# A decoder trunk on one core: the Strassen chunks of the down projections are loaded once, split and summed in one place

## The chip, the cores and the metric

The kernel runs on one core of a Trainium2 chip, which has eight. The metric is the device time of one execution in microseconds. The engines that matter are PE (matrix products), DVE (elementwise arithmetic), ACT (copies and activations) and SP, which only issues transfers from memory. Each engine runs its own list of instructions in the order in which the program emitted them.

## The reference

Two layers over 256 tokens of width 1024, in float32. Each layer has a token mixer (a chunked gMLP in the first, block attention in the second), a normalization, a gated feed-forward with a causal convolution, and a second normalization. The change lies in the feed-forward's last product, the down projection:

```python
def conv_ffn(x, w_up, conv_w, conv_b, w_down):
    S = x.shape[1]
    h = x @ w_up                       # 256 x 1024 times 1024 x 5632
    hp = jnp.pad(h, ((0, 0), (CONV_WIDTH - 1, 0), (0, 0)))
    hc = conv_b
    for j in range(CONV_WIDTH):
        hc = hc + conv_w[j] * hp[:, j:j + S]
    g, val = jnp.split(hc, 2, axis=-1)
    return (jax.nn.gelu(g) * val) @ w_down     # 256 x 2816 times 2816 x 1024
```

## The kernel before

**Products.** Every float32 operand is split into two parts, a high part `hi` in the matmul's own format (a copy by ACT) and a low part `lo`, the rest (a subtraction by DVE); `split` (L339) records the two. A product is the sum of three matmuls: hi times hi, hi times lo, lo times hi. All weights come from memory, are split on arrival and used once. So each chunk of weights costs a transfer, ACT copies and DVE subtractions, then PE time.

**Chunks.** `stream` (L349) lists all weight chunks in the order of use: `f_up0` (22 chunks), `f_dn0` (11), the attention's, `f_up1` (22), `f_dn1` (11). A chunk is 128 partitions x 2048 columns (1 MB); a chunk of a down projection holds two slices k = 2c and 2c + 1 of the contraction, 1024 output columns each. `prep(i)` (L470) records a chunk's load into one of two `raws` tiles and its splits into `whi` and `wlo`, rings that hold five chunks. `spent(name, c)` (L500) is called when chunk c has been used and calls `prep` for the chunk five further on.

**The Strassen chunks.** In each down projection four chunks, 3, 5, 6 and 7 (`FAST`, L54), are multiplied by `unit` (L706) in Strassen's way. The chunk is a 2 x 2 matrix of blocks (B11, B12 are the halves of slice 2c, B21, B22 of slice 2c + 1), the tokens are two halves, and seven block products (21 matmuls of 512 columns) stand for eight (24). They need
- the plain blocks B11 and B2 (B21 and B22 together), split into `whi`, `wlo`: for these `prep` loads 512 and 1024 columns of the chunk into a `raws` tile;
- four sums of blocks, the weight forms: `load_sums` (L431) loads the whole chunk a second time, into two places of the scratch tile `ff` (0 to 1023 and 2560 to 3583 for the first and third of the four, 1024 to 2047 and 3584 to 4607 for the second and fourth), and `weight_forms` (L438) adds blocks there in place (one DVE instruction of 1024 elements, two of 512) and splits the four sums into the `xt` tiles (first and third) or into used-up columns of `rr` (second and fourth). When it is done it records the load of the chunk two further on, into the same place;
- sums of token blocks, `token_forms` (L459), in `small`.

The scratch tile `ff` also serves `conv_up` (L891), the up projection with its gate: `joined` (2560 and 3584, 1024 columns each, in turn) and `grings` (0 to 2047) hold a pass's values, two chunks in a pass, until its result is split into `rr`.

**Order.** `project_out` (L683) goes through chunks 0 to 7 in order, both token tiles in each, and through the last three chunks (`TAIL`) one output piece after another: 18 matmuls, six slices, for each of the four pieces. The forms of chunk 3 are recorded at its start, those of chunks 5 and 6 after chunk 3, those of 7 after chunk 5 (`more`, L764). `combine` (L741) adds the products that belong to the units once chunk 7 is done. `ln_rows` (L541) loads the scale and shift rows of the next normalization into the one tile `lnrow`, at the start of the projection; the tile also holds the attention's values later.

**The planner.** Nothing is issued while this is recorded. `Plan` (L84) collects operations with estimated costs, the buffers that they read and write, and a due time worked back from PE's order; `emit` (L129) runs a list schedule with those costs (a load lands 1100 ns plus its bytes at 415 GB/s after its issue) and then emits every engine's instructions in the order of start times. So the costs and due times fix the order of DVE, ACT and SP beforehand, while the real waits are those of semaphores. PE's main products keep the order in which they were recorded.

Of the kernel before, what the change touches and what calls it, by code (L numbers as in the profile page):

```python
# [18 lines left out]
P = 128  # L19
# [32 lines left out]
REST = 25000  # L52
AHEAD = 12000
FAST = {"f_dn0": (3, 5, 6, 7), "f_dn1": (3, 5, 6, 7)}  # L54

# [173 lines left out]
def trunk_kernel(ctx: ExitStack, tc: tile.TileContext, a: dict, out: bass.AP):  # L231
# [25 lines left out]
    def place(which, at, cols):  # L257

        t = rr if which == "rr" else ff
        prev = [b for s, e, b in owners[which] if s < at + cols and at < e]  # L260
        b = Buf(t[:, at:at + cols], prev)
        owners[which] = [x for x in owners[which] if not (at <= x[0] and x[1] <= at + cols)] + [(at, at + cols, b)]
        return b
# [61 lines left out]
    def tt(o, x, y, op, r, w):  # L325
        dve(70 + 1.04 * flat(x), lambda: nc.vector.tensor_tensor(o, x, y, op=op), r, w)  # L326
# [8 lines left out]
    def load(o, src, w, r=(), nbytes=None, rank=None):  # L335
        nbytes = nbytes or flat(o) * P * 4
        plan.op("sp", nbytes / 415.0, lambda: nc.sync.dma_start(o, src), r, w, nbytes=nbytes, rank=rank)
# [38 lines left out]

    xrows = [Buf(t) for t in xs_]

    def raw_of(i):
        if i == 2:  # L380
            early = place("ff", 2560, CH)
        elif i == 3:
            return [(b, b.ap, 0) for b in xrows]
        else:
            early = raws.new()
        return [(early, early.ap[:, s * SUB:(s + 1) * SUB], s * 4) for s in range(2)]
# [4 lines left out]
    def used_up(k0, k1):  # L391

        if "spare" in inner:
            inner["spare"] = [Buf(b.ap, [b]) for b in inner["spare"]]
            return inner["spare"]
        bufs = []
        for b in inner["rr"]:
            n = Buf(b.ap[:, k0 * S:k1 * S], [Buf(None)])
            n.prev[0].ops = [o for k in range(k0, k1) for o in [b.wr[k], *b.rd.get(k, ())]]
            bufs.append(n)  # L400
        inner["spare"] = bufs
        return bufs
# [22 lines left out]
    def is_fast(i):  # L425
        name, c = stream[i]
        return c in FAST.get(name, ())

    raw_sums = {}

    def load_sums(name, j):  # L431

        key = name, FAST[name][j]
        raw_sums[key] = [place("ff", o + SUB * (j % 2), SUB) for o in (0, 5 * HALF)]
        for n, b in enumerate(raw_sums[key]):
            load(b.ap, a[name][key[1]][:, n * SUB:(n + 1) * SUB], [(b, range(2))])

    def weight_forms(name, j):  # L438

        key = name, FAST[name][j]  # L440
        r0, r1 = raw_sums[key]
        f = ff.rearrange("p (a n) -> p a n", n=HALF)
        b11 = 2 * (j % 2)
        b12, b21, b22 = b11 + 1, b11 + 5, b11 + 6
        h, l = xt_new() if j % 2 == 0 else used_up(0, KT)
        tt(f[:, b22:b12 - 1:-5, :], f[:, b12:b12 + 1, :].to_broadcast([P, 2, HALF]),
           f[:, b22:b11 - 1 if b11 else None:-6, :], ALU.add, [(r0, [0, 1]), (r1, [1])], [(r0, [1]), (r1, [1])])
        tt(f[:, b11, :], f[:, b22, :], f[:, b11, :], ALU.add, [(r0, [0]), (r1, [1])], [(r0, [0])])
        tt(f[:, b21, :], f[:, b11, :], f[:, b21, :], ALU.add, [(r0, [0]), (r1, [0])], [(r1, [0])])
        for n, raw in ((1, r1), (0, r0)):  # L450
            parts, sl = [2 * n, 2 * n + 1], slice(n * SUB, (n + 1) * SUB)
            split((h, parts, h.ap[:, sl]), (l, parts, l.ap[:, sl]), (raw, [0, 1], raw.ap))
        forms[key] = h, l
        if j + 2 < len(FAST[name]):
            load_sums(name, j + 2)

    tokens = {}

# [11 lines left out]
    def prep(i):  # L470
        name, c = stream[i]
        raw = raw_of(i)
        if is_fast(i):
            for o, n in ((0, HALF), (SUB, SUB)):
                load(raw[0][0].ap[:, o:o + n], a[name][c][:, o:o + n], [(raw[0][0], range(o // 256, (o + n) // 256))])
        elif name != "a_v":
            load(raw[0][0].ap, a[name][c], [(raw[0][0], range(8))])
        for _, _, s, e in [h for h in HEAD if h[:2] == (name, c)]:
            b, v, p0 = raw[s // SUB]
            o = s % SUB  # L480
            load_head(v[:, o:o + e - s], [(b, range(p0 + o // 256, p0 + (o + e - s) // 256))], name, c, s)
        subs = []
        for s in range(2):
            hi, lo = whi.new(), wlo.new()
            rb, rv, p0 = raw[s]
            pieces = [(0, HALF)] if is_fast(i) and not s else [(0, 256), (256, 512), (512, 1024)] if not i + s else [(0, 512), (512, 1024)] if name == "a_v" or i in FINE else [(0, SUB)]
            for b, e in pieces:
                split((hi, range(b // 256, e // 256), hi.ap[:, b:e]), (lo, range(b // 256, e // 256), lo.ap[:, b:e]),
                      (rb, range(p0 + b // 256, p0 + e // 256), rv[:, b:e]))
            subs.append((hi, lo))  # L490
        chunks[i] = subs
# [8 lines left out]
    def spent(name, c):  # L500
        i = where[name, c] + CHUNKS
        if i < len(stream):
            prep(i)
# [10 lines left out]
    def xt_new():  # L514
        return xth.new(), xtl.new()
# [166 lines left out]

    def project_out(name, nk, at, xold, li, rows_i, wait=REST, first=None):  # L683

        rows = None if name == "b_o" else ln_rows(rows_i)
        last, fine = li is None, name not in ("a_out", "f_dn0", "b_o")


# [68 lines left out]
                done_with(b, 0)  # L757

        if units:
            load_sums(name, 0)  # L760
            if len(units) > 1:
                load_sums(name, 1)
            weight_forms(name, 0)
        def more(c):  # L764

            for j, after in enumerate([None, KT // 2 - 1, *units[:2]]):
                if c == after and j < len(units):
                    weight_forms(name, j)

        for k, t in order:  # L770
            if k // 2 in units:
                if k % 2 == t == 0:
                    unit(k // 2)
                elif k % 2 and t:
                    spent(name, k // 2)
                    more(k // 2)
                    if k // 2 == units[-1]:
                        combine()
                continue
            step(t, k, pieces[t][:1])  # L780
            step(t, k, pieces[t][1:], last=nk - 1 if t == 0 or not fine else nk - NARROW - 1)
            if t and k % 2:
                spent(name, k // 2)
                if units:
                    more(k // 2)
# [106 lines left out]
    def conv_up(layer, h, l):  # L892
# [50 lines left out]
        for i in range(2, FT, 2):  # L943
            whole, four = four_banks()
            cols_times([(b, *sub(name, i + j // 2, j % 2)) for j, b in enumerate(four)], h, l)
            for n in range(2):
                spent(name, i + n)
            c = joined.new()
            c3, b3 = (x.rearrange("p (a n) -> p a n", a=4) for x in (c.ap, whole))
            act(c3, b3[:, :, S:], AF.Copy, four, [c], psum=True)  # L950
            tt(c3, b3[:, :, :S], c3, ALU.add, [*four, c], [c])
            gv = [r.new() for r in grings]
            for n in range(2):
                for j in range(2):
                    o, d = c3[:, 2 * n + j, :], gv[j].ap[:, n * S:(n + 1) * S]
                    cw, dp = cc[:, layer, j * FT + i + n, :], (gv[j], [n])
                    act(d, o, AF.Identity, [c, convc], [dp], bias=cw[:, 3:4], scale=cw[:, 2:3])
                    for e in (1, 2):
                        stt(d[:, e:], o[:, :S - e], cw[:, 2 - e:3 - e], d[:, e:], ALU.mult, ALU.add, [c, dp, convc], [dp])
            key, both = (f"f_dn{layer}", i // 2), [0, 1]  # L960
            g = gv[0]
            if key[1] in FAST.get(key[0], ()):
                g = kept[key] = place("ff", 4608 + HALF * (FAST[key[0]].index(key[1]) % 3), HALF)
            act(g.ap, gv[0].ap, AF.Gelu_apprx_tanh, [(gv[0], both)], [(g, both)], table="gelu")
            tt(g.ap, g.ap, gv[1].ap, ALU.mult, [(g, both), (gv[1], both)], [(g, both)])
            at = slice(i * S, (i + 2) * S)
            split((ah, [i, i + 1], ah.ap[:, at]), (al, [i, i + 1], al.ap[:, at]), (g, both, g.ap))
            if key in kept and key[1] in FAST[key[0]][:2]:
                token_forms(key)
        return lambda k, t: (av[:, k, t * P:(t + 1) * P], lv[:, k, t * P:(t + 1) * P], [(ah, [k]), (al, [k])])  # L970


# [221 lines left out]
```

## Time and profile before

| what | value |
|---|---|
| median of three runs | 563.64 us (563.34 to 566.98) |
| the profiled execution's own time | 569.39 us |
| its span | 567.7 us |
| busy PE, DVE, ACT | 553.3, 509.2, 374.8 us |
| moved by DMA | 117.40 MB |
| f_up0's last matmuls end, f_dn0 begins | 202.4 us |
| f_up1's last matmuls end, f_dn1 begins | 496.8 us |

How to read it: times are microseconds from the start of the span. A row of the timeline or of the chain gives start, length, engine, line of the kernel, operation, destination, source and the number of instructions; in brackets stands how long the engine had been idle before it and what released it. A row of a window gives, for each engine, busy time and in brackets the number of instructions that touch the window, then the clock that PE was granted (1.00 is full), the share of the DMA engines' time, and GB/s. A row of a wait gives total, number and longest. In the rows of groups the mean length of one instruction, in ns, stands behind the busy total. Most operations are recorded by helpers: L308 is every product, L320 ACT's copies and activations, L326 DVE's additions and subtractions, L330 its fused operations, L337 a load on the SP queue, L314 a transposition.

### The profile page before, as it was taken

The numbers are of one execution on the slowest core, as the hardware profiler recorded it, in microseconds if no ns is written. First come the engines' busy times: TensorE is split into PE (matmuls) and PEld (weight loads), VectorE is DVE, ScalarE is ACT, GpSimd is POOL, SyncE is SP. The second block draws the span as 40 slices with busy tenths as digits, with TensorE's granted clock in tenths as the row PEclk, the third lists the DMA queues.
The fourth block names the chain that finished last, engine by engine and source line by source line (L and its number), as shares of the span: only waits on it lengthen the run. The fifth ranks groups of instructions, "written<-read, shape, count | busy, mean of one in ns | idle before, by whom it ended". The sixth has DMA issues, their size and how long they took to land.

```text
span 567.7 us, 8102 instructions
## 1 busy us (share of the span) xinstructions
PE 553.3 (97%) x2959; PEld 470.8 (83%) x2959; DVE 509.2 (90%) x891; ACT 374.8 (66%) x627; POOL 11.8 (2%) x17
## 2 busy tenths in 40 slices
PE   8999999999999999999999999999999999999794
PEld 6888888998988988778888887788898898988684
DVE  5898899999999998998958888889999999997987
ACT  6746678688787772555667877487787778673510
POOL 0110010000000000001000000000000000000001
PEclk9999999999999999989999999999999999999888
DMA  8986545775545557574475544426766455566602
GB/s 319 405 297 252 177 145 218 276 291 199 199 152 219 204 190 268 173 260 148 162 282 186 186 169 149 185 82 234 285 253 222 180 218 196 169 214 214 207 13 74
DMA packets 23559, 117.40 MB, mean 207 GB/s; under 512 B 2640, under 2 KB 5984, under 8 KB 12384
## 3 DMA queue, kind: packets, MB, share of 16 engines
q1 hardware_dynamic: 22944, 116.24, 56.6%
q10 hardware_dynamic: 576, 0.66, 0.3%
q8 instruction: 23, 0.38, 0.2%
q14 instruction: 16, 0.13, 0.1%
HBM read 115.81 MB, written 1.07 MB: 206 GB/s over the span
## 4 chain that ended last, share of the span: by engine, by line
PE 78%; DVE 9%; DMA 8%; issue 3%; ACT 2%; SPq 0%; DVEq 0%; ACTq 0%
PE bank L308 75%; DMA ff<-in_f_dn 5%; DVE ff L326 4%; PE bank L314 2%; DMA raw<-in_f_dn 2%; DVE wlo L326 2%; DVE ff L330 1%; DVE rr L326 1%; ACT whi L320 1%; DMA raw<-in_head 1%; ACT xt L320 0%; DVE x L330 0%; DVE xt L326 0%; ACT rr L320 0%; DVE small L326 0%
## 5 line engine op out<-in xcount | busy, mean ns | idle before, releaser
L320 ACT ACTIVATE whi<-raw 128x1024 fp32r<-128x1024 f32 (+2 forms) x209 | 188.0, 935 | 87.0 <-DMA raw<-in_f_dn 28.6
L326 DVE TENSOR_TENSOR wlo<-raw,whi 128x1024 fp32r<-128x1024 f32 (+2 forms) x209 | 217.5, 1069 | 17.4 <-ACT whi L320 16.4
L308 PE MATMUL bank<-xt,whi 128*128 128x512 f32 x832 | 195.8, 391 | 0.0
L308 PEld LDWEIGHTS bank<-xt,whi 128*128 128x128 f32 x832 | 154.2, 188 | 30.7
L308 PE MATMUL bank<-whi,rr 128*128 128x512 f32 (+1 forms) x392 | 125.5, 391 | 3.3 <-DVE rr L326 3.3
L308 PE MATMUL bank<-xt,wlo 128*128 128x256 f32 x832 | 104.7, 283 | 0.0
L308 PEld LDWEIGHTS bank<-xt,wlo 128*128 128x128 f32 x832 | 103.0, 192 | 2.1
L308 PEld LDWEIGHTS bank<-whi,rr 128*128 128x128 f32 x392 | 73.6, 189 | 18.9 <-DVE rr L326 4.0
L308 PE MATMUL bank<-wlo,rr 128*128 128x512 f32 (+1 forms) x196 | 76.0, 388 | 0.0
L330 DVE SCALAR_TENSOR_TENSOR ff<-ff,convc 128x255 f32<-128x255 f32 (+1 forms) x160 | 67.1, 478 | 0.1
L308 PE MATMUL bank<-whi,xt 128*128 128x512 f32 (+1 forms) x196 | 62.4, 400 | 1.1 <-ACT whi L320 1.1
L326 DVE TENSOR_TENSOR ff<-ff 128x512 f32<-128x512 f32 (+3 forms) x76 | 45.0, 615 | 8.4 <-DMA ff<-in_f_dn 8.4
L320 ACT ACTIVATE ff<-bank 128x256 f32<-128x256 f32 (+3 forms) x66 | 39.6, 617 | 19.3 <-PE bank L308 19.0
L320 ACT ACTIVATE ff<-ff,convc 128x256 f32<-128x256 f32 x80 | 42.3, 591 | 13.8 <-DVE ff L326 13.1
L308 PEld LDWEIGHTS bank<-whi,xt 128*128 128x128 f32 x196 | 37.6, 196 | 9.6 <-ACT whi L320 2.1
L308 PEld LDWEIGHTS bank<-wlo,rr 128*128 128x128 f32 x196 | 37.1, 189 | 7.3
L326 DVE TENSOR_TENSOR ff<-bank,ff 128x256 f32<-128x256 f32 (+2 forms) x50 | 37.5, 769 | 1.8 <-ACT ff L320 1.8
L308 PE MATMUL bank<-wlo,xt 128*128 128x512 f32 (+1 forms) x98 | 36.9, 392 | 0.0
L320 ACT ACTIVATE rr<-ff 128x512 fp32r<-128x512 f32 (+2 forms) x36 | 24.5, 692 | 15.7 <-DVE ff L326 15.7
L320 ACT ACTIVATE ff<-bank,lncol 128x128 f32<-128x128 f32 x48 | 18.8, 459 | 17.5 <-PE bank L314 17.4
L326 DVE TENSOR_TENSOR rr<-ff,rr 128x512 fp32r<-128x512 f32 (+2 forms) x36 | 27.4, 773 | 1.4 <-ACT rr L320 1.4
L326 DVE TENSOR_TENSOR xt<-ff,xt 128x256 fp32r<-128x256 f32 (+2 forms) x31 | 21.6, 702 | 2.3 <-ACT xt L320 2.0
(70 smaller groups left out, 373.8 us busy)
## 6 DMA issues: line engine op xcount, KB each, us to landing
raw<-in_f_up SPq DMA_DIRECT2D x44, 1024.0 KB, 4.8
raw<-in_f_dn SPq DMA_DIRECT2D x14, 1024.0 KB, 4.9
ff<-in_f_dn SPq DMA_DIRECT2D x16, 512.0 KB, 4.7
raw<-in_b_qk SPq DMA_DIRECT2D x8, 1024.0 KB, 4.8
lnrow<-in_lnrow SPq DMA_DIRECT2D x5, 1024.0 KB, 6.6
raw<-in_a_u SPq DMA_DIRECT2D x4, 1024.0 KB, 8.5
raw<-in_a_out SPq DMA_DIRECT2D x4, 1024.0 KB, 5.1
raw<-in_f_dn SPq DMA_DIRECT2D x8, 512.0 KB, 4.7
```

Of the source, the lines that this page charges most:

```text
L308: nc.tensor.matmul(o, l, x, start=start, stop=stop, skip_group_check=mixed)
L314: nc.tensor.transpose(o, x, ident.ap)
L320: plan.op("act", ns, lambda: nc.scalar.activation(o, x, func, **kw), r, w, table=table)
L326: dve(70 + 1.04 * flat(x), lambda: nc.vector.tensor_tensor(o, x, y, op=op), r, w)
L330: lambda: nc.vector.scalar_tensor_tensor(o, x, s, y, op0=op0, op1=op1), r, w)
```

## The change

Each of the eight Strassen chunks is loaded once, in two halves of 512 KB, into a home of its own; the plain blocks are split from there, and the sums are then formed in place there. `HOMES` names the home of each of the four: the place of ff that held the first and third chunk's copy, the one of the second and fourth, the tile `lnrow`, and the first one again. So chunk 3 lies in home 0, chunk 5 in home 1, chunk 6 in `lnrow`, chunk 7 in home 0 once chunk 3's forms are split. `prep` records these loads; `load_sums` is gone. `FORMS` says for each of the four which tiles take its forms and after which chunk they are recorded; both are as before. The first sum, which overwrites B12 and B22, waits until B22's plain split has read; the sum over B11 waits for B11's. The rows of the second normalization are loaded after `combine` is recorded instead of at the projection's start. In `conv_up` the two calls of `spent` stand at the end of a pass instead of after its products.

```diff
+HOMES = (0, 1, 2, 0, 1)
+FORMS = ((0, None), (1, 3), (0, 3), (1, 5))
...
+    def home(i):
+        name, c = stream[i]
+        j = HOMES[FAST[name].index(c)]
+        if j < 2:
+            pair, t, at = [place("ff", o + SUB * j, SUB) for o in (0, 5 * HALF)], ff, (0, 1, 5, 6)
+            at = [x + 2 * j for x in at]
+        else:
+            old, t, at = rowring.held[0], rowring.tiles[0], (0, 1, 2, 3)
+            group = rowring.held[0] = Buf(old.ap, [old])
+            pair = [Buf(old.ap[:, n * SUB:(n + 1) * SUB], [old]) for n in range(2)]
+            for b in pair:
+                b.ops = group.ops
+        raw_sums[name, c] = pair, t.rearrange("p (a n) -> p a n", n=HALF), at
+        return [(b, b.ap, 0) for b in pair]
+
     def raw_of(i):
+        if is_fast(i):
+            return home(i)
...
-    def load_sums(name, j):
-        key = name, FAST[name][j]
-        raw_sums[key] = [place("ff", o + SUB * (j % 2), SUB) for o in (0, 5 * HALF)]
-        for n, b in enumerate(raw_sums[key]):
-            load(b.ap, a[name][key[1]][:, n * SUB:(n + 1) * SUB], [(b, range(2))])
...
     def weight_forms(name, j):
         key = name, FAST[name][j]
...
-        h, l = xt_new() if j % 2 == 0 else used_up(0, KT)
+        (r0, r1), f, (b11, b12, b21, b22) = raw_sums[key]
+        left, right, both = (range(2), range(2, 4), range(4))
+        h, l = used_up(0, KT) if FORMS[j][0] else xt_new()
...
         forms[key] = h, l
-        if j + 2 < len(FAST[name]):
-            load_sums(name, j + 2)
...
         if is_fast(i):
-            for o, n in ((0, HALF), (SUB, SUB)):
-                load(raw[0][0].ap[:, o:o + n], a[name][c][:, o:o + n], [(raw[0][0], range(o // 256, (o + n) // 256))])
+            for n, (b, _, _) in enumerate(raw):
+                load(b.ap, a[name][c][:, n * SUB:(n + 1) * SUB], [(b, range(4))])
...
-        rows = None if name == "b_o" else ln_rows(rows_i)
+        rows = None if name == "b_o" or name in FAST else ln_rows(rows_i)
...
         if units:
-            load_sums(name, 0)
-            if len(units) > 1:
-                load_sums(name, 1)
             weight_forms(name, 0)
...
                     if k // 2 == units[-1]:
                         combine()
+                        rows = ln_rows(rows_i)
...
             cols_times([(b, *sub(name, i + j // 2, j % 2)) for j, b in enumerate(four)], h, l)
-            for n in range(2):
-                spent(name, i + n)
             c = joined.new()
...
                 token_forms(key)
+            for n in range(2):
+                spent(name, i + n)
```

More of the change, by code (lines that the diff above doesn't have):

```diff
@@ L377, in trunk_kernel @@
     xrows = [Buf(t) for t in xs_]
+    raw_sums = {}
+    def home(i):
[12 more added lines that the diff above has]
+        return [(b, b.ap, 0) for b in pair]
     def raw_of(i):
+        if is_fast(i):
+            return home(i)
         if i == 2:
@@ L427, in is_fast @@
         return c in FAST.get(name, ())
-    raw_sums = {}
-    def load_sums(name, j):
-        key = name, FAST[name][j]
-        raw_sums[key] = [place("ff", o + SUB * (j % 2), SUB) for o in (0, 5 * HALF)]
-        for n, b in enumerate(raw_sums[key]):
-            load(b.ap, a[name][key[1]][:, n * SUB:(n + 1) * SUB], [(b, range(2))])
     def weight_forms(name, j):
         key = name, FAST[name][j]
[L441 to L444, printed above, removed]
-        h, l = xt_new() if j % 2 == 0 else used_up(0, KT)
[L446 to L449, printed above, removed]
+        (r0, r1), f, (b11, b12, b21, b22) = raw_sums[key]
+        left, right, both = (range(2), range(2, 4), range(4))
+        h, l = used_up(0, KT) if FORMS[j][0] else xt_new()
+        tt(f[:, b22:b12 - 1:b12 - b22, :], f[:, b12:b12 + 1, :].to_broadcast([P, 2, HALF]),
+           f[:, b22:b11 - 1 if b11 else None:b11 - b22, :], ALU.add, [(r0, both), (r1, right)], [(r0, right), (r1, right)])
+        tt(f[:, b11, :], f[:, b22, :], f[:, b11, :], ALU.add, [(r0, left), (r1, right)], [(r0, left)])
+        tt(f[:, b21, :], f[:, b11, :], f[:, b21, :], ALU.add, [(r0, left), (r1, left)], [(r1, left)])
         for n, raw in ((1, r1), (0, r0)):
             parts, sl = [2 * n, 2 * n + 1], slice(n * SUB, (n + 1) * SUB)
-            split((h, parts, h.ap[:, sl]), (l, parts, l.ap[:, sl]), (raw, [0, 1], raw.ap))
+            split((h, parts, h.ap[:, sl]), (l, parts, l.ap[:, sl]), (raw, both, raw.ap))
         forms[key] = h, l
-        if j + 2 < len(FAST[name]):
-            load_sums(name, j + 2)
     tokens = {}
@@ L759, in project_out @@
         if units:
-            load_sums(name, 0)
-            if len(units) > 1:
-                load_sums(name, 1)
             weight_forms(name, 0)
         def more(c):
-            for j, after in enumerate([None, KT // 2 - 1, *units[:2]]):
-                if c == after and j < len(units):
+            for j, (_, after) in enumerate(FORMS[:len(units)]):
+                if c == after:
                     weight_forms(name, j)
```

## The prediction, on record before the change was run

> **What bounds the kernel now.** I read the page's busy shares first, then the windows of each down projection, cut where its stages change, then the PE rows at the two places where PE stops, then the chain that ended last behind those stops, and last what DVE and the SP queue wait for there.
>
> ```profile
> PE 553.3 (97%) x2959; PEld 470.8 (83%) x2959; DVE 509.2 (90%) x891; ACT 374.8 (66%) x627; POOL 11.8 (2%) x17
> ```
>
> PE is busy nearly throughout, DVE is close behind. An average of 97% hides stages, so here are the stages of f_dn0 (first four rows) and f_dn1 (last four): chunks 0 to 2, chunks 3 to 6, the unit of chunk 7, the rest.
>
> ```profile
> core 0: us, PE busy (x) PEld busy (x) DVE busy (x) ACT busy (x) POOL busy (x), PEclk, DMA share, GB/s
> 202.38:218.70 16.32, 16.32 (x73) 13.51 (x72) 15.70 (x23) 10.15 (x14) 0.00 (x0) 1.00 0.67 223
> 218.70:238.42 19.72, 19.72 (x88) 16.33 (x87) 15.81 (x22) 8.12 (x10) 0.00 (x0) 1.00 0.60 193
> 238.42:247.41 8.99, 7.13 (x23) 4.63 (x22) 8.76 (x10) 6.73 (x8) 0.00 (x0) 0.81 0.80 288
> 247.41:264.60 17.19, 17.19 (x81) 14.29 (x80) 16.42 (x26) 8.37 (x15) 1.35 (x1) 1.00 0.49 182
> 496.81:513.13 16.32, 16.32 (x73) 13.51 (x72) 15.63 (x23) 10.27 (x14) 0.00 (x0) 1.00 0.66 219
> 513.13:532.85 19.72, 19.72 (x88) 16.33 (x87) 14.67 (x20) 7.79 (x9) 0.00 (x0) 1.00 0.53 178
> 532.85:543.89 11.04, 7.70 (x22) 5.78 (x21) 11.04 (x14) 7.13 (x8) 0.00 (x0) 0.69 0.56 190
> 543.89:560.55 16.66, 16.63 (x85) 14.09 (x83) 13.55 (x25) 0.00 (x0) 1.05 (x1) 1.00 0.09 32
> ```
>
> Chunks 0 to 2 are 72 matmuls in 16.32 us: 0.2267 us each. A unit has 21, so 4.76 us, an ordinary chunk 24, so 5.44; chunks 3 to 6 are then 4.76 + 5.44 + 4.76 + 4.76 = 19.72, just what both windows show: no loss up to there. Chunk 7's unit should take 4.76 and takes 8.99 and 11.04. PE loses 4.23 us in f_dn0 and 6.28 in f_dn1, 10.51 together; the rest of the two projections runs at pace. What happens in that unit:
>
> ```profile
> 238.88 0.39 PE L308 MATMUL bank<-whi,rr 128*128 128x512 f32 x1
> 240.24 0.50 PE L308 MATMUL bank<-whi,small 128*128 128x512 f32 x1 [0.97 <-ACT small L320]
> 240.57 0.40 PE L308 MATMUL bank<-wlo,small 128*128 128x512 f32 x1
> 241.85 0.61 PE L308 MATMUL bank<-whi,small 128*128 128x512 f32 x1 [0.89 <-DVE small L326]
> 242.25 0.63 PE L308 MATMUL bank<-whi,rr 128*128 128x512 f32 x1
> 242.68 0.63 PE L308 MATMUL bank<-wlo,rr 128*128 128x512 f32 x1
> ```
>
> ```profile
> 536.81 0.80 PE L308 MATMUL bank<-whi,rr 128*128 128x512 f32 x1 [3.35 <-DVE rr L326]
> ```
>
> PE stands 0.97 + 0.89 = 1.86 us for chunk 7's token forms, and 3.35 us in f_dn1 for DVE work. After either, matmuls start 0.43 us apart (242.25 to 242.68), not 0.23: the windows' PEclk falls to 0.81 and 0.69. So 4.23 is 1.86 of standing and 2.37 of slow clock, 6.28 is 3.35 and 2.93. The chain that ended last says why DVE is late, first for f_dn0, then f_dn1:
>
> ```profile
> 216.25 0.69 DVE rr L326
> ...
> 217.01 6.25 DMA ff<-in_f_dn
> ...
> 230.54 4.53 DMA ff<-in_f_dn
> ...
> 235.16 1.23 DVE ff L326
> ```
>
> ```profile
> 510.40 0.69 DVE rr L326
> ...
> 511.15 7.00 DMA ff<-in_f_dn
> ...
> 524.98 5.04 DMA ff<-in_f_dn
> ...
> 536.81 23.73 PE bank L308 x103
> ```
>
> The load that lands at 235.06 and at 530.02 is the second copy of chunk 7. It could not be issued before the forms of chunk 5, which held the same place of ff, were split; DVE then still has 6.7 us of chunk 7's sums, splits and other work before PE may go on. Meanwhile DVE had stood idle for such loads (199 to 248.8, then 493 to 544.1):
>
> ```profile
> DVE ff L326 <- DMA ff<-in_f_dn: 3.2, 3, 1.9
> DVE rr L326 <- ACT rr L320: 0.7, 1, 0.7
> DVE xt L326 <- ACT xt L320: 0.6, 1, 0.6
> ```
>
> ```profile
> DVE ff L326 <- DMA ff<-in_f_dn: 5.2, 4, 2.5
> DVE rr L326 <- ACT rr L320: 0.3, 1, 0.3
> ```
>
> So DVE idles 4.5 and 5.5 us ahead of stalls of 1.86 and 3.35.
>
> **The change, part by part.** *Loads removed.*
>
> ```profile
> ff<-in_f_dn SPq DMA_DIRECT2D x16, 512.0 KB, 4.7
> ...
> raw<-in_f_dn SPq DMA_DIRECT2D x8, 512.0 KB, 4.7
> ...
> raw<-in_f_dn SPq DMA_DIRECT2D x8, 256.0 KB, 5.2
> ```
>
> The 16 raw loads go (6 MB of 117); the 16 others stay, four of them with lnrow for their place. In time by itself: 0, since PE waits for no such load directly; it thins the traffic in which the 512 KB ahead of 223.26 and 518.15 took 6.25 and 7.00 us against a median of 4.7, worth 0 to 2.3 us of landing. I count 0.
>
> *Loads moved.* Chunk 6 goes to the lnrow tile, free long before, and its load can be issued before the stage. Chunk 7 goes to chunk 3's place, so it may start when chunk 3's forms are split, not chunk 5's. In the trace the place of chunk 3 is refilled (by chunk 6) from the issues at 211.70 on, that of chunk 5 at 229.40:
>
> ```profile
> 211.70 5.64 SPq L337 DMA_DIRECT2D ff<-in_f_dn  x4
> 217.39 2.24 SPq L337 DMA_DIRECT2D raw<-in_f_dn  x3
> 229.40 1.46 SPq L337 DMA_DIRECT2D ff<-in_f_dn  x2
> ```
>
> Chunk 7 thus lands some 12 us earlier, before 223.3, and its sums can fill the holes of DVE. This is the gain: up to 10.51.
>
> *Plain splits moved behind the homes.* Chunks 3, 5 and 7 lose their own raw tiles: their plain splits and sums share one landing, and the sums wait until the plain splits have read. The prices:
>
> ```profile
> L326 DVE TENSOR_TENSOR wlo<-raw,whi 128x1024 fp32r<-128x1024 f32 x152 | 181.4, 1218 | 14.0 <-ACT whi L320 13.0 <-PE bank L308 0.5
> L326 DVE TENSOR_TENSOR wlo<-raw,whi 128x512 fp32r<-128x512 f32 x55 | 35.5, 681 | 1.4 <-ACT whi L320 1.3
> ```
>
> Chunk 5 is the tight one. Its second half lands early (the last gate gives up that place once the convolution has read it), the first as before at 223.26. Behind that come the wide sum 1.22, the plain split of 512 columns 0.68, two sums 0.68 each, about 1.1 for ACT (taken as DVE's wide row), and two splits 1.22 each: 223.26 + 6.8 = 230.1. The unit of chunk 5 starts at 218.70 + 4.76 + 5.44 = 228.90, and its thirteenth matmul needs the last of this at 231.6: 1.5 us to spare. In f_dn1 518.15 + 6.8 = 524.9 against 526.1. I count 0; from below it could not gain, from above it costs what lies past that margin.
>
> Chunk 3's plain splits, 1.22 + 0.68 = 1.9 us, now wait for the first landing of the stage; DVE did them before it. That opens a hole of 0 (the last gate's arithmetic fills it) to 1.9 us; I take 1.2.
>
> *Order of SP, rows of lnrow.* The norm rows now load behind chunk 6's forms:
>
> ```profile
> 525.47 2.35 DVE L326 TENSOR_TENSOR xt<-ff,xt 128x1024 fp32r<-128x1024 f32 x2
> ...
> 553.95 2.74 DVE L330 SCALAR_TENSOR_TENSOR x<-x,stat,lnrow 128x512 f32<-128x512 f32 x4
> ```
>
> From 527.8 to 553.95 there are 26 us for 1 MB, under 10 even in the traffic above: 0. Without that cover the last normalization would wait the landing out. On SP, waits of the homes stand ahead of the chunk 8 to 10 and b_v loads; those need earlier splits on DVE anyway. The later prep in the up projection only alters the recording order, not what a load waits for: 0, since PE shows no loss there.
>
> *The sum.* If DVE never stood, the last split of chunk 10 would end 4.5 and 5.5 us earlier than in these rows:
>
> ```profile
> 246.57 2.36 DVE L326 TENSOR_TENSOR wlo<-raw,whi 128x1024 fp32r<-128x1024 f32 x2 [0.23 <-ACT whi L320]
> ```
>
> ```profile
> 539.54 4.62 DVE L326 TENSOR_TENSOR wlo<-raw,whi 128x1024 fp32r<-128x1024 f32 x4
> ```
>
> That is 244.4 and 538.7. An unstalled PE ends chunk 7 at 243.18 and 537.61 and wants the second half of chunk 10 fifteen matmuls later, at 246.6 and 541.0. DVE may therefore idle 2.2 and 2.3 us per stage at no cost. I expect 1.2 for the start, 0.8 for ACT's lead (0.3 to 1.3 before) and 0.8 for landings (0 to 3.2 or 5.2): 2.8, so a stop of about 0.5 in each. A stop may cost more than itself: 0.9 us stops brought 2.37 of slow clock. For a 0.5 us stop no row exists; between 0 and 2.4 I take 0.5, nearer to nothing because it will be split over chunks 8 to 10. Left over: 1.0 per stage. Gain 10.51 - 2.0 = 8.5 us.
>
> The Trainium skill (TensorE: Matmul & The Clock Gate, Part 1, What's actually happening) has the clock fall to half only after an idle window of about 3.4 us. The rows above disagree: two stops under 1 us were enough. By that rule small stops cost only themselves, and the sum would be 10.51 - 1.0 = 9.5.
>
> The profiled execution took 569.39 us, its span 567.7; the runs' median is 563.64, 5.75 less. Where that lies isn't shown. If all of it were in these two stops, the runs would lose only 4.8 us there; if none, the full 10.5. I take the gain as it stands, since a uniform part fits as well: 569.39 to 560.9, and **563.64 to 555.1**.
>
> **The rivals.** *DVE still last in one or both stages* (0.30). For: DVE is at 8.76 of 8.99 and 11.04 of 11.04 us in the stalled windows, and the spare is 2 us. Against: 8 us of its waits are for just the loads that move. If idle time comes to 3.5 us in a stage, PE stands 1.3 and the clock adds 2.4: 3.7, so that f_dn0 gains 0.5 and f_dn1 2.1. One such stage costs 2.7 over the forecast, 557.8; both, 561.0.
>
> *The stop only moves* (0.14): chunk 10's raw tile is freed by chunk 8's split, so its load may be the next late thing, or the runs have little stall. Against it: chunk 8's data no longer queue behind chunk 7's copy. Time: 562 to 564, gain under 2.
>
> *Slower* (0.06): DVE runs in order, and the planner fixes that order by its own landing times. If it puts chunk 5's first sum ahead of chunks 6 and 7, DVE stands from 216.9 to 223.26 and from 511.1 to 518.15, 6.3 and 7.0 us, besides the 1.2 at the start. PE then loses 7.5 - 2.2 + 2.37 = 7.7 and 8.2 - 2.3 + 2.93 = 8.8 in place of 4.23 and 6.28: 6.0 more, 569.6. It decides from 4.1 us of idle time in f_dn0 and 5.6 in f_dn1. Against: work of chunk 6, whose data is there, is ready in that hole.
>
> **How the numbers follow.** The forecast has 0.50, with its own range 552.5 (all of 10.51 and a little) to 558. The rivals reach up; cutting the slower one and half of the third, the range is 552.5 to 562.5. One per cent, 5.6 us, is about what a measurement tells here. Faster by more: nearly all of the forecast, and half of the first rival, 0.47 + 0.17 = 0.64. Slower by more: most of the last, 0.05. Within: 0.31.
>
> **What would show it.** Right: chunk 7's unit at 4.8 to 5.8 us in both projections, PEclk 1.00 in that window, no DMA piece of f_dn in the chain after chunk 5's landing, DVE's waits for f_dn loads down from 8.4 us to under 3, 111 MB moved. Wrong: a PE wait over 0.9 us at chunk 5 (the shared home), at chunks 8 to 10 (DVE or the raw tile), or PE at pace through both projections with a time that stays: then the stops were the profiled execution's.

## The result, and the profile after

| | kernel before | changed kernel | ratio, 95% interval |
|---|---|---|---|
| first measurement, 9 runs each | 563.67 us | 560.82 us | 0.9928 (0.9902 to 0.9955) |
| again, in a later job | 565.49 us | 560.21 us | 0.990 (0.9864 to 0.9937) |
| profiled executions: own time, span | 569.39, 567.7 us | 561.77, 560.0 us | |

The change gains 0.7 to 1.0%, some 3 to 5 us, where 8.5 were forecast. From profile to profile it is 7.6 us of own time. That difference is the first thing to explain. The ratios here and below leave out two runs that lie far off, one of the kernel before at 782 us and one of a variant at 1945 us.

The windows of the changed kernel's f_dn0 and f_dn1, cut as before into chunks 0 to 6 and the unit of chunk 7:

```profile
202.23:238.27 36.04, 36.04 (x160) 29.82 (x159) 33.42 (x44) 23.07 (x29) 0.00 (x0) 1.00 0.42 139
238.27:245.26 6.99, 5.42 (x22) 3.80 (x22) 6.91 (x8) 3.52 (x5) 0.00 (x0) 1.00 0.59 196
494.39:530.43 36.04, 36.04 (x161) 29.84 (x159) 34.40 (x45) 23.61 (x29) 0.00 (x0) 1.00 0.39 132
530.43:536.25 5.82, 5.09 (x22) 3.86 (x21) 5.63 (x7) 3.01 (x4) 0.00 (x0) 1.00 0.53 180
```

Chunks 0 to 6 still take 36.04 us, with no loss (before, 16.32 + 19.72). Chunk 7's unit takes 6.99 and 5.82 us, against 4.76 at pace: PE loses 2.23 and 1.06 us where it lost 4.23 and 6.28. The granted clock stays at 1.00. The three places where PE stands, two in f_dn0 and one in f_dn1:

```profile
240.35 0.50 PE L310 MATMUL bank<-whi,small 128*128 128x512 f32 x1 [0.73 <-DVE small L328]
...
242.62 0.72 PE L310 MATMUL bank<-rr 128*128 128x512 f32 x2 [0.84 <-DVE rr L328]
...
533.59 0.74 PE L310 MATMUL bank<-rr 128*128 128x512 f32 x2 [0.73 <-DVE rr L328]
```

Standing adds up to 1.57 us in f_dn0 and 0.73 in f_dn1, so 0.66 and 0.33 us are lost beyond it, some 0.3 per stop, with the clock at 1.00.

What DVE waited for in f_dn0, and then in f_dn1:

```profile
DVE wlo L328 <- ACT whi L322: 1.7, 3, 1.2
DVE rr L328 <- ACT rr L322: 0.5, 1, 0.5
DVE ff L328 <- DMA ff<-in_f_dn: 0.3, 1, 0.3
```

```profile
DVE wlo L328 <- ACT whi L322: 1.3, 2, 1.2
DVE ff L328 <- ACT ff L322: 0.4, 1, 0.4
```

Chunk 7's data is there early: ACT starts on its plain parts at 220.45 us, where before its sums had to wait until 235.06.

```profile
220.45 1.58 ACT L322 ACTIVATE whi<-ff 128x512 fp32r<-128x512 f32 x2 [3.68 <-DMA ff<-in_f_dn]
```

DVE's direct waits for these loads are all but gone, 0.3 us for 8.4, and its idle time ahead of the stop is 2.5 and 1.7 us for 4.5 and 5.5. So what sets the stop now? The chain that ended last, from the landing of chunk 5 on (pieces of the chain: start, length, what):

```profile
216.46 7.74 DMA ff<-in_f_dn
...
229.11 2.36 DVE rr L328 x2
231.47 2.27 DVE xt L328 x2
233.74 0.60 DVE wlo L328
234.34 2.28 DVE ff L328 x4
...
237.96 1.14 DVE wlo L328
239.09 0.60 DVE ff L328
239.69 0.60 DVE small L328
240.29 2.28 DVE rr L328 x2
```

From 229 us it is DVE without a hole: forms of chunk 5 (rr), of chunk 6 (xt), chunk 7's last plain split and sums, chunk 8's two splits, and only then chunk 7's token parts (small) and forms (rr), at which PE stands. DVE's timeline has the two splits of chunk 8, 2.3 us of work that chunk 7 does not need:

```profile
236.53 1.23 DVE L328 TENSOR_TENSOR wlo<-raw,whi 128x1024 fp32r<-128x1024 f32 x1
...
237.87 1.23 DVE L328 TENSOR_TENSOR wlo<-raw,whi 128x1024 fp32r<-128x1024 f32 x1
```

### The profile page after: what moved, and what is told of

It is laid out like the page before. It is cut to its first block, busy times and chain, and to the rows that moved or that the text cites. A ratio compares the mean times of both kernels' runs of the same rounds, so it can differ in the third digit from the quotient of the medians.

```text
span 560.0 us, 8045 instructions
## 1 busy us (share of the span) xinstructions
PE 549.2 (98%) x2959; PEld 468.2 (84%) x2959; DVE 508.7 (91%) x891; ACT 376.1 (67%) x627; POOL 11.9 (2%) x17
## 2 busy tenths in 40 slices
DMA packets 21256, 111.11 MB, mean 198 GB/s; under 512 B 2385, under 2 KB 5729, under 8 KB 10081
## 4 chain that ended last, share of the span: by engine, by line
PE 60%; DVE 27%; DMA 8%; issue 3%; ACT 2%; POOL 0%; DVEq 0%; SPq 0%; ACTq 0%
PE bank L310 58%; DVE wlo L328 9%; DVE ff L328 6%; DVE ff L332 5%; DMA raw<-in_f_up 3%; DMA ff<-in_f_dn 3%; DVE rr L328 2%; PE bank L316 2%; DVE xt L328 1%; ACT whi L322 1%; DMA raw<-in_f_dn 1%; DVE x L332 1%; DMA raw<-in_head 1%; DVE x L328 1%; DVE lnrow L328 1%
## 5 line engine op out<-in xcount | busy, mean ns | idle before, releaser
L328 DVE TENSOR_TENSOR wlo<-raw,whi 128x1024 fp32r<-128x1024 f32 (+2 forms) x193 | 203.0, 1083 | 15.9 <-ACT whi L322 12.1
L322 ACT ACTIVATE whi<-raw 128x1024 fp32r<-128x1024 f32 (+2 forms) x193 | 174.3, 943 | 58.7 <-DMA raw<-in_f_up 28.4
L310 PE MATMUL bank<-whi,rr 128*128 128x512 f32 (+1 forms) x392 | 124.2, 387 | 0.0
L328 DVE TENSOR_TENSOR ff<-ff 128x512 f32<-128x512 f32 (+3 forms) x70 | 40.9, 600 | 0.6 <-DMA ff<-in_f_dn 0.3
L310 PEld LDWEIGHTS bank<-wlo,xt 128*128 128x128 f32 x98 | 19.0, 197 | 3.6
```

What stands on the lines that cost most here:

```text
L310: nc.tensor.matmul(o, l, x, start=start, stop=stop, skip_group_check=mixed)
L322: plan.op("act", ns, lambda: nc.scalar.activation(o, x, func, **kw), r, w, table=table)
```

## The experiments

All ratios are to the kernel before in the same job; the four jobs ran on four chips, where its median was 565.2 to 565.7 us. "Unit losses" are what PE loses against 4.76 us in chunk 7's unit, in f_dn0 and in f_dn1, in the one profiled execution.

| kernel | median us | ratio (95% interval) | unit losses us |
|---|---|---|---|
| before, once more | 565.49 | 0.9999 (0.997 to 1.0028) | 3.64, 4.86 |
| two copies, new places | 560.24 | 0.9897 (0.9862 to 0.9932) | 1.60, 1.03 |
| one copy, old places | 564.13 | 0.9976 (0.995 to 1.0002) | 4.32, 1.49 |
| changed, chunk 10 in ff | 560.16 | 0.9891 (0.9851 to 0.9932) | 1.48, 0.06 |
| changed, once more | 560.21 | 0.990 (0.9864 to 0.9937) | 1.45, 1.06 |
| one copy, chunk 6 alone moved | 558.63 | 0.9871 (0.983 to 0.9912) | 0.59, 1.03 |
| changed, chunk 8's low parts on POOL | 567.9 | 1.0039 (1.0013 to 1.0065) | 0.16, 0.06; stops at chunk 5, see below |
| changed, 1.1 us more on DVE | 562.45 | 0.9945 (0.9913 to 0.9976) | 2.66, 1.71 |
| changed, chunk 5's load first | 559.0 | 0.9893 (0.9866 to 0.992) | 0.58, 2.14 |
| chunk 6 moved, chunk 10 in ff | 558.71 | 0.9892 (0.9865 to 0.992) | 0.77, 0.0 |
| chunk 5's load first, chunk 10 in ff | 559.05 | 0.9898 (0.987 to 0.9927) | 0.0, 0.69 |
| two copies, chunk 6 alone moved | 561.31 | 0.9923 (0.9895 to 0.9951) | 2.91, 0.93 |

**How steady is the stop of the kernel before?** The kernel before, with no edit.

> The kernel before, unchanged, profiled once more. Theory A (the stop at chunk 7 has no fixed length, and the first profile caught a long one): the units of chunk 7 lose other amounts than 4.23 and 6.28 us, together about 5 to 8, the runs' times spread by 3 us or more, and the slower runs show the lower mean clock. Theory B (the loss is a steady 10.5 us, and the runs' shorter time lies elsewhere): both units lose 4 and 6 us again, whatever the run's time.

The profiled execution took 565.77 us. PE's stops in f_dn0, then the windows of both units:

```profile
238.01 0.50 PE L308 MATMUL bank<-whi,small 128*128 128x512 f32 x1 [1.04 <-ACT small L320]
...
239.63 0.50 PE L308 MATMUL bank<-whi,small 128*128 128x512 f32 x1 [0.88 <-DVE small L326]
...
241.90 0.74 PE L308 MATMUL bank<-rr 128*128 128x512 f32 x2 [0.84 <-DVE rr L326]
```

```profile
236.13:244.53 8.40, 5.64 (x23) 3.71 (x21) 8.18 (x10) 6.16 (x8) 0.00 (x0) 1.00 0.82 283
530.63:540.25 9.62, 6.66 (x22) 5.04 (x21) 9.62 (x11) 6.87 (x8) 0.00 (x0) 0.82 0.54 211
```

In f_dn0 PE stands longer than in the first profile, 1.04 + 0.88 + 0.84 = 2.76 us against 1.86, and yet the granted clock stays at 1.00 and 3.64 us are lost, not 4.23; again some 0.3 us per stop come on top of the standing, 0.88 in all. In f_dn1 it stands 2.96 us, the clock is 0.82, 4.86 are lost, not 6.28. So 8.5 us in all against 10.51: theory A. The runs say how usual either is: of 69 runs of the kernel before in the first three jobs, 7 have a mean clock of 0.987 or less and take 567.2 to 571.9 us, 569.4 on average; the other 62 average 565.4. The execution behind the prediction had 0.987 and 569.39. The changed kernel's sixteen runs lie between 0.992 and 0.998.

**The changed kernel once more**, beside the second batch.

> The changed kernel, unchanged, beside the others on one chip. Theory A (the stop before has no fixed length, 3 to 10 us in both units together, and the changed kernel still stops 3 us): ratio to the kernel before 0.988 to 0.994, the units of chunk 7 at 5.5 to 7 us, mean clock 0.996 to 0.998 in all runs. Rival (the change costs something ahead of f_dn0, which begins at 202.2 us in its profile against 200 us in three others): f_dn0 begins at 202 us again, and the ratio is worse than that of the two copies in the new places, 0.990.

0.990 and units of 6.21 and 5.82 us are theory A's; the mean clocks are 0.992 to 0.998, two of the seven under the 0.996 that it wanted. f_dn0 begins at 202.14 us again, which the rival wanted, but the ratio equals that of the two copies (next), whose f_dn0 begins at 199.91. The lag arises in the first 20 us, which the change doesn't touch: 66 matmuls there in both profiles of the changed kernel, 65 and 76 in those of the kernel before, 75 to 77 in those of all variants. How often the changed kernel's other runs start late isn't known.

**Places or copies?** First two copies in the new places, then one copy in the old places. In the first, `prep` loads the plain blocks as before, and the second copy is loaded by

```diff
+    def load_sums(name, j):
+        c = FAST[name][j]
+        for n, (b, _, _) in enumerate(home(where[name, c])):
+            load(b.ap, a[name][c][:, n * SUB:(n + 1) * SUB], [(b, range(4))])
...
         if units:
+            for j in range(3):
+                load_sums(name, j)
             weight_forms(name, 0)
+            load_sums(name, 3)
```

> Two copies of each Strassen chunk as before, but the second copy goes to the new places (chunk 6 to lnrow, chunk 7 to chunk 3's place), and the norm rows load late. Theory 1 (the earlier landing of chunks 6 and 7 is what gains): as the changed kernel, 560 to 562 us, chunk 7 lands before 225 us, its unit at 5 to 7 us. Theory 2 (fewer transfers and freed raw tiles gain): 563 to 565 us, as before, with 117 MB moved.

0.9897, the units lose 1.60 and 1.03: as the changed kernel, though 117.40 MB are moved. The second needs chunk 7's `prep` recorded after chunk 5's forms, whose place it takes:

```diff
-HOMES = (0, 1, 2, 0, 1)
+HOMES = (0, 1, 0, 1)
...
+                    if k // 2 == units[0]:
+                        more(k // 2)
+                        spent(name, 2)
+                        spent(name, k // 2)
```

> One copy of each Strassen chunk, but in the old places: chunk 6 in chunk 3's, chunk 7 in chunk 5's. Theory 1: chunk 7 lands after chunk 5's forms again, at about 235 us, and now its plain splits wait too, so its unit loses more than before, 6 us and 8 us: 565 to 569 us. Theory 2: 561 us or less, since 6 MB are gone.

0.9976, an interval that touches 1: not slower, as theory 1 had it, and not 561 either. In f_dn0 DVE waits 2.9 us for one ff load, and the unit loses 4.32, at a granted clock of 0.81; in f_dn1 DVE waits for none and the unit loses 1.49. The load is not chunk 7's: the instruction that waits, at 218.11 us, is chunk 5's first sum, and with chunk 6 in its old place nothing fills the hole ahead of it.

```profile
DVE ff L328 <- DMA ff<-in_f_dn: 2.9, 1, 2.9
```

The places carry most of the gain; the copies alone at most half a per cent, perhaps nothing.

**Which of the two moves?** One copy, chunk 6 in lnrow, chunk 7 in chunk 5's place (`HOMES = (0, 1, 2, 1)`, with the recording order of the last kernel).

> The changed kernel with one move undone: chunk 6 in lnrow, but chunk 7 in chunk 5's place, recorded after chunk 5's forms. If chunk 7's early landing is what gains (theory 1): like the one copy in the old places, ratio 0.996 to 1.000, chunk 7 landing at about 235 us with DVE waiting 2 to 4 us for it. If emptying DVE's hole with chunk 6 is enough: 0.990 to 0.993.

0.9871, and 558.63 us is the lowest median of all. Theory 1, which rested on chunk 7's early landing, falls: chunk 7's load is issued at 224.02 us here, as chunk 5's forms are split, lands by 229.73, and DVE does not wait for it: of the waits below, the one for a load is chunk 5's. (The landing is still 3.4 us earlier than before, 29.3 us after the start of f_dn0 against 32.7, since chunk 5's forms are done earlier; in the changed kernel it is 18.2. Chunk 7's move alone was not run.)

```profile
224.02 1.46 SPq L339 DMA_DIRECT2D ff<-in_f_dn  x2
```

```profile
DVE wlo L328 <- ACT whi L322: 1.1, 3, 0.5
DVE ff L328 <- DMA ff<-in_f_dn: 0.4, 1, 0.4
DVE rr L328 <- ACT rr L322: 0.3, 1, 0.3
```

DVE idles 1.8 us in f_dn0, with chunk 6's plain splits in the former hole. And chunk 5's first sum runs earlier: at 218.07 us, 17.6 after the start of f_dn0, against 224.22, 22.0 after it, in the changed kernel. The rows of this run, then those of the changed kernel:

```profile
212.33 2.46 DVE L328 TENSOR_TENSOR xt<-ff,xt 128x1024 fp32r<-128x1024 f32 x2
...
215.85 1.82 DVE L328 TENSOR_TENSOR wlo<-lnrow,whi 128x1024 fp32r<-128x1024 f32 x2
218.07 1.23 DVE L328 TENSOR_TENSOR ff<-ff 128x1024 f32<-128x1024 f32 x1 [0.40 <-DMA ff<-in_f_dn]
```

```profile
213.42 1.23 DVE L328 TENSOR_TENSOR xt<-ff,xt 128x1024 fp32r<-128x1024 f32 x1
214.56 1.23 DVE L328 TENSOR_TENSOR wlo<-raw,whi 128x1024 fp32r<-128x1024 f32 x1
215.69 0.70 DVE L328 TENSOR_TENSOR rr<-ff,rr 128x512 fp32r<-128x512 f32 x1
...
224.22 1.23 DVE L328 TENSOR_TENSOR ff<-ff 128x1024 f32<-128x1024 f32 x1 [0.32 <-DMA ff<-in_f_dn]
```

Half of the 4.4 us is DVE's order: chunk 5's last half waits for the split of the last gate's result (rr), which stands ahead of chunk 3's splits (xt) here, at 211.73, and behind them in the changed kernel, at 215.69, so it is issued 12.0 us after the start of f_dn0 (at 212.49) against 14.2 (at 216.46). The other half is the landing, 5.5 us here against 7.74 in the changed kernel, where chunk 7's 1 MB as well as chunk 8's goes out ahead of it. So the run differs from the changed kernel in more than chunk 7's place: the planner chose another order.

The same move with two copies kept (`load_sums(name, 3)` after chunk 5's forms):

> Two copies of each Strassen chunk as before; the one move that is left is chunk 6's second copy, in lnrow (and the norm rows late); chunk 7's second copy stays in chunk 5's place. Theory 4 (chunk 6's own place is what gains: DVE gets work for the hole in which it waited, and chunk 5's landing has no transfer ahead of it): ratio 0.987 to 0.991, units of chunk 7 at 5 to 6.5 us. Rival (chunk 6's place gains only together with one copy, since two copies leave the traffic and the raw tiles as they were): 0.994 to 1.000.

0.9923, between the two. Chunk 6's place alone gives about 0.8%; one copy may add to it (0.9871), but the intervals overlap.

**Does the order of those two loads matter?** The changed kernel with one edge more for the planner:

```diff
+                if c == 5:
+                    five[name] = plan.ops[-1]
+                if c == 7:
+                    plan.ops[-1].deps.add(five[name])
```

> The changed kernel, with one order changed on SP: chunk 7's load is issued behind chunk 5's, not ahead of it. Theory 3 (in the changed kernel chunk 7's early transfer delays the landing of chunk 5, which DVE then waits for): chunk 5's second load lands within 6 us of its issue in place of 7.7, DVE waits under 1.9 us in f_dn0, units of chunk 7 at 5.0 to 5.8 us, ratio 0.985 to 0.989 as with chunk 7 in chunk 5's place (0.987). Rival (that kernel gained by the planner's other order, not by the landing): as the changed kernel, 0.990 to 0.993.

In f_dn0 ACT starts chunk 5's last plain part 17.8 us after the stage begins, and the unit loses 0.58; in f_dn1 the landing still takes 6.76 us and the unit loses 2.14. 0.9893 fits both theories; it decides nothing.

**Is DVE's queue what is left?** In the changed kernel one low part of chunk 7 is subtracted twice:

```diff
+                if stream[i] in TWICE and s:
+                    tt(lo.ap[:, b:e], rv[:, b:e], hi.ap[:, b:e].bitcast(F32), ALU.subtract,
+                       [(rb, range(p0 + b // 256, p0 + e // 256)), (hi, range(b // 256, e // 256))], [(lo, range(b // 256, e // 256))])
```

> The changed kernel, but one low part of chunk 7 (1024 columns) is subtracted twice: 1.1 us more of DVE in each projection. Theory 1b (DVE's queue sets the stop): units of chunk 7 longer by about 1 us each, 2 to 3 us in all, up to 5 where the clock falls. Rival (landings or ACT set it, DVE has room): within 0.5 us of the changed kernel.

562.45 against 560.21 in the same job, 2.2 us for two instructions of 1.1, and 1.9 us more lost in the two units: DVE's queue sets the stop, nearly one for one. (The intervals of the two ratios overlap a little; the units' losses do not rest on them.) The order in it can be changed: chunk 8's splits go early because chunk 10's load waits for their raw tile. Here chunk 10 goes to chunk 5's place instead (the third scratch piece of `combine` moves out of its way):

```diff
+        if stream[i] in TEN:
+            return [(b, b.ap, 0) for b in (place("ff", o + SUB, SUB) for o in (0, 5 * HALF))]
```

> The changed kernel, but chunk 10 loads into chunk 5's place of ff when that is free, and no longer into the raw tile that chunk 8's splits free. Theory 1 (what is left of the stop at chunk 7 is DVE's order: chunk 8's splits, 2.3 us, stand ahead of chunk 7's forms because chunk 10's load waits for them): the units of chunk 7 fall from 7.0 and 5.8 us to 4.8 to 5.3, and the time by 1.5 to 3 us, to 558 to 559. Rival (DVE's amount of work is the bound): PE stops at chunks 8 to 10 by as much instead, 560 to 561 us.

The f_dn1 unit is at pace, 4.82 us, as theory 1 had it; DVE's chunk 8 splits stand behind chunk 7's forms there. The f_dn0 unit still loses 1.48, where one of the two splits (at 236.16 us) stays ahead of them, and the time is not told from the changed kernel's. With the other edits it goes further:

> Chunk 6 in lnrow, chunk 7 in chunk 5's place, and chunk 10 in chunk 3's place in ff instead of the raw tile that chunk 8's splits free. If the rest of the stop (0.6 and 1.0 us with chunk 10 in the raw tile) is DVE's order, chunk 8's splits ahead of chunk 7's forms: units of chunk 7 at 4.8 to 5.0 us, 1 to 1.6 us less than 558.6, ratio 0.983 to 0.986. If DVE's amount is the bound, the stop goes to chunks 8 to 10 and the ratio stays at 0.986 to 0.989.

> Both edits on the changed kernel: chunk 7's load behind chunk 5's, and chunk 10 in chunk 5's place of ff once that is free. If landing and order add up: ratio 0.982 to 0.986, both units of chunk 7 under 5.2 us. If DVE's amount is the bound: 0.986 to 0.990, with PE stops at chunks 9 and 10 of 0.2 to 1 us.

In each of the two, one unit is at pace and the other loses 0.7 to 0.8; of the stops at chunks 9 and 10 that the rival expects only one of 0.17 us shows. Yet the ratios are 0.9892 and 0.9898, what the changed kernel reaches with more loss. With 2 to 3 us left to win, these ratios, whose intervals are 3 us wide, can't rank the variants.

**POOL for the low parts of chunk 8.** `split(..., by="pool")` with `nc.gpsimd.tensor_tensor` in place of DVE's.

> The changed kernel, but the two low parts of chunk 8 are subtracted by POOL, not DVE: 2.3 us less of DVE in each projection, ahead of chunk 7's forms. Theory 1b (what is left of the stop is DVE's queue, with chunk 8's splits ahead of chunk 7's forms): units of chunk 7 at 4.8 to 5.3 us, 2 to 3 us less, 558 us or ratio 0.985 to 0.988. Rival (the remaining stop is latency, from landing to ACT to DVE, or POOL slows DVE as it works beside it): no less than the changed kernel.

567.9 us, slower than before by 0.4%. DVE's rows, then POOL's:

```profile
221.19 2.90 DVE L329 TENSOR_TENSOR lnrow<-lnrow 128x512 f32<-128x512 f32 x1
224.01 3.43 DVE L329 TENSOR_TENSOR ff<-ff 128x1024 f32<-128x1024 f32 x1
```

```profile
221.05 5.31 POOL L350 TENSOR_TENSOR wlo<-raw,whi 128x1024 fp32r<-128x1024 f32 x2 [141.81 <-ACT whi L323]
```

While POOL runs, DVE's sum of 512 takes 2.90 us in place of 0.69, that of 1024 takes 3.43 in place of 1.23: 4.4 us lost to save 2.3. The delay falls on chunk 5, where PE now stands 2.12 us in f_dn0 and 1.8 in f_dn1 for ACT's copy of its forms, and then 0.8 in each for DVE's split. Chunk 7's unit, to which PE now comes later, runs nearly at pace, 4.92 and 4.82 us.

## Why the prediction was right and wrong, step by step

- **The place of the loss, right.** Chunk 7's units, and DVE's lateness behind them; chunks 0 to 6 at pace before and after.
- **The size of the loss, wrong; this is the step that failed.** "I take the gain as it stands, since a uniform part fits as well": the 10.51 us came from an execution 5.75 us above the median, and the whole gain worked out from it was carried over to the runs. The second profiled execution, whose 565.77 us lie at the runs' median, loses 8.50 us in the two units, 2.0 less. The 3.6 us between the two executions are these 2.0 and 2.3 ahead of f_dn0, less 0.7 elsewhere. So the other half of that paragraph, a loss of 4.8 us if all of the excess lay in the stops, was too low. What fails is the step from one execution to the runs: from profile to profile the forecast was close, 569.39 - 8.5 = 560.9 against 561.77, and these two executions start f_dn0 within 0.2 us of each other.
- **The clock term, mis-read in part.** The 2.37 + 2.93 us that the sum put down to slow clock do not come with every stop: the clock stayed at 1.00 in f_dn0 of the second profile. And by the 0.3 us per stop that are lost at a clock of 1.00, some 0.6 of the 2.37 and 0.3 of the 2.93 (an estimate) were not clock.
- **What is left over, too small.** Forecast 1.0 us per stage, at chunks 8 to 10; measured 2.23 and 1.06, then 1.45 and 1.06, at chunk 7. DVE's idle time was about as forecast or less, 2.5 and 1.7 against 2.8. But the spare of 2.2 us was worked out for chunk 10, as if DVE served whatever PE needs next; the planner had put chunk 8's 2.3 us ahead of chunk 7's forms. Something like the 0.5 put down to the clock did come, 0.66 and 0.33, but with the clock at 1.00.
- **8.5 forecast, 3 to 5 measured.** With the second profile of the kernel before and the first of the changed one, the units gain 8.50 - 3.29 = 5.2 us. Against the forecast 10.51 - 2.0, the loss before is 2.0 smaller and what is left over 1.3 larger. The later job gives 5.3, the first measurement 2.9. In the first the kernel before took 1.8 us less and the changed kernel 0.6 more than in the later one; why isn't shown.
- **Chunk 7's early landing, right but not what most of the gain needs.** It lands by 220.45 instead of 235.06. The gain comes as well with the landing at 229.73, by chunk 6's place, which the prediction used only as work for DVE's holes. That the early transfer goes out ahead of chunk 5's was not priced. It costs no stop at chunk 5, but the margin of 1.5 us there is used up: the last split of its forms ends at 231.47, when the unit's thirteenth matmul starts. And it delays everything on DVE behind.
- **The signs.** Four of the five signs of being right came: the clock of 1.00, no f_dn load in the chain after chunk 5's landing, 0.3 us of waits, 111.11 MB. The fifth did not: a unit of 4.8 to 5.8 us in both stages, where 6.99 and 5.82 were measured. What came, a stop that stays at chunk 7, is not among the signs of being wrong.
- **Loads removed, counted at 0: not contradicted.** One copy in the old places gives 0.2% with an interval that holds 0.
- **Chunk 3's later splits, the norm rows, the later prep: no loss to be seen.** The norm rows load at 524.74 and are first read at 546.31.
- **The rivals.** What happened is the first, DVE last in both stages, priced at 561.0; the time is 560.8. Its mechanism was right, but that the time agrees is luck: it came from 3.5 us of idle time and a slow clock, and neither was there; the stop came from the order of DVE's queue, and the rest from the smaller loss before. The slower case did not come: chunk 6's work filled the hole.

## What to carry to other kernels

Before a stall is turned into a gain, ask whether the profiled execution is a typical one: when its own time stands 1% above the median, the stall you look at may be where that lies, and the gain scales with the usual stall, not with the one in view. A resource that runs without holes behind the landing is the next bound; its spare has to be counted in the order in which its queue really stands, up to the first thing the waiting engine needs. When several buffers move at once, try each move alone: here the one that looked secondary carries most of the gain, and the one that looked decisive was never run alone.

## What the runs showed of the hardware

- **The clock after a stop is not a function of its length.** 1.86 us of standing in two pieces brought 0.81 over the unit, 2.76 in three pieces left it at 1.00, 2.96 and 3.35 in one piece brought 0.82 and 0.69. The Trainium skill (TensorE: Matmul & The Clock Gate, Part 1, What's actually happening) tells of a window of 3413 ns that runs freely, whatever the kernel does; the row of 2.76 us agrees with its rule that a full idle window is needed, the rows of 1.86, 2.96 and 3.35 us, all shorter than the window, do not. That the phase of the window explains the difference was not tried.
- **DVE and POOL don't add up.** A POOL subtraction of 128x1024 takes 2.7 us, and DVE's two-operand instructions beside it lose as much as 2.2 us each. The Trainium skill (SBUF — State Buffer, Who interferes with whom) states it: a DVE instruction with two SBUF inputs contends with a GpSimd instruction that reads SBUF. The rows above agree.
- **The start drifts.** f_dn0 begins at 199.8 to 202.4 us over the profiles of all these kernels, the kernel before at 202.38 and 200.09. In the two profiles of the kernel before, PE runs 21 and 33 matmuls in the first 10 us, with the same clock of 1.00 in the row:

```profile
0.00:10.00 10.00, 8.08 (x21) 5.63 (x22) 4.37 (x10) 4.97 (x9) 0.70 (x6) 1.00 0.80 277
```

```profile
0.00:10.00 10.00, 9.16 (x33) 6.35 (x34) 4.68 (x10) 5.25 (x9) 0.70 (x6) 1.00 0.78 276
```

Four matmuls of 256 columns take 1.22 us at 6.53 in the first profile and 0.68 at 5.35 in the second, so PE was slow for longer in the first, though the row's clock doesn't show it. Two us of any comparison of single profiles can come from there.
